# A gated encoder block on one core: z's forms loaded ahead of the last head's y_r, whose share goes out by accumulating stores

## The chip, the cores and the metric

One Trainium2 chip, one of its cores. The metric is the device time of one execution in microseconds: the median of the runs. All times inside an execution are counted from the start of its profiled span. Engines are called by their names or by the profile's short forms: TensorE (PE, with PEld for its weight loads), VectorE (DVE), ScalarE (ACT), GpSimd (POOL), SyncE (SP). Transfers started by POOL go through one queue, emptied in order, that the profile calls software_dynamic; those started by SP go through the one called hardware_dynamic.

## What is computed

One layer of an encoder block on x of 512 tokens by 1024 features, all in float32. Cut to what matters here:

```python
h = rmsnorm(x, g_mix)
xc, gb, gc, q, k, v, g_sw, gate_a, gate_r = split(h @ w_in)
y_a = (gb * dwconv3(gc * xc)) @ w_a_out                     # z = gb * conv
ret = retention(q, k, v)                                    # 4 heads, 512 wide each, both directions
y_r = (groupnorm(ret) * g_ret * silu(g_sw)) @ w_r_out       # 2048 rows: 512 of each head
merged = sigmoid(gate_a) * y_a + sigmoid(gate_r) * y_r
x = x + merged @ w_o
x = x + swiglu(rmsnorm(x))                                  # then a last rmsnorm
```

y_r is a sum over four heads, each of which contributes its own product with 512 rows of `w_r_out`.

## The kernel before

Every float32 operand is split into a high and a low part (`split`: the high part is a rounding copy on ScalarE, L167 or L170; the low part is a subtraction on VectorE, L168 or L171), and every product is three matmuls (high·high, high·low, low·high). The weights pass through the same split on their way: a load on SP into a raw tile (L204, L228), for some a sum of two raw tiles on VectorE (L240), the copy, the subtraction. `take()` hands the next split unit to the product and prefetches the units behind it. The order of all weights is fixed by a list, `PLAN`.

Several products, among them y_a = z · w_a_out, are done by a Strassen-like scheme (`strassen`, L375 to 399): seven products of quarter matrices (24 matmuls of 128x512 each, all at L365), in the order a11, s1, s2, a12, s3, a22, s4. Three pairs of banks are used: `a`, `d` and `b`; a holds a11, then a11 + s2 (s2's product adds to it), and so on. Between them stand copies to SBUF (`snap`, L372, ScalarE): p1 is the copy of a after a11, u2 the one after s2, u3 the one after s3. Each product does its first unit of weights for both tiles of tokens, then its second. The left operands (z's forms: a11, a12, s1 to s4, a22, high and low) were written to DRAM by `z_forms` long before, and are loaded back into tiles of the pool `big` named `zform`.

The heads run in a loop (L802 to 817): the product of scores with v (`do_pv`), a group norm, a transposition on VectorE (`do_t`, L181), and one head late the head's share of y_r, `do_wr(h - 1)`. That is two products (`half` 0 and 1, the left and right 512 columns), each of 48 matmuls (L280 to L282) into four banks. Of heads 0 to 2 each bank is copied to a tile by ScalarE (`snap`) and stored by POOL into `yrd[half]` in DRAM, from head 1 on with `accum_op=ALU.add`, so that the DMA adds to what is there (L788). Ahead of the last head's share the sum so far is loaded (L822), after it z's forms (L827) and the gate of A (`sga`, L832), all by POOL. The gate of R (`sgr`) was loaded by SP (L815). The last head's products are evicted by VectorE (`ev_last`): the bank is added to the sum (L792), which is multiplied by `sgr` (L793). Then comes the y_a product, whose four evictions merge: times `sga` (L840), plus the finished R part (L841). `turn` then transposes a half of the merged rows on TensorE (L851) and splits it, and w_o's product (L280 to L282 again) reads the split.

Three pools matter. `big` has 14 buffers of 1 MB; `tmp` has nine tiles of 128x512, from which every `snap` takes one, and a tile is free again when its last reader is done, for a stored one when the store has landed; PSUM has eight banks. The instructions of an engine run in the order in which a scheduler put them when the kernel was built. A wait at the head of an engine's queue holds all behind it. POOL's transfers use eight counters in turn, and each waits until the transfer that last used its counter has landed.

Of the kernel before, what the change touches and what calls it, by code (L numbers as in the profile page):

```python
# [12 lines left out]
F32 = mybir.dt.float32  # L13
F32R = mybir.dt.float32r
AF = mybir.ActivationFunctionType
ALU = mybir.AluOpType

P = 128
# [4 lines left out]
HEADS = 4  # L23
# [115 lines left out]
def block_kernel(ctx: ExitStack, tc: tile.TileContext, xT, xtok, wpack, wquad, cols, decs, rot, g_ffn, g_final, out):  # L139
    nc = tc.nc  # L140

    const = ctx.enter_context(tc.tile_pool(name="const", bufs=1))
    big = ctx.enter_context(tc.tile_pool(name="big", bufs=14))
# [11 lines left out]
    def bigtile(dt=F32, n=4):  # L155
        return big.tile([P, n, 512], dt, tag="big", name="big", padded_shape=[P, 4, 512])
# [4 lines left out]
    def bank():  # L161
        return psum.tile([P, 512], F32, tag="bank", name="bank")
# [115 lines left out]
    def mm3(ps, left, right, first, last):  # L278
        (lh, ll), (rh, rl) = left, right
        nc.tensor.matmul(ps, lh, rh, start=first, stop=False)  # L280
        nc.tensor.matmul(ps, lh, rl, start=False, stop=False)  # L281
        nc.tensor.matmul(ps, ll, rh, start=False, stop=last)  # L282

    def act_pair(tiles, k, sl=slice(0, S)):
        hi, lo = tiles
        return hi[k // 4][:, k % 4, sl], lo[k // 4][:, k % 4, sl]
# [10 lines left out]
    def token_major(lhs, row0, chunks, evict, before=None):  # L297


        pss = [bank() for _ in range(NB)]  # L300
        n = 4 * chunks
        for kk in range(n):
            if kk % 4 == 0:
                c = Chunk()
            if before:
                before(kk)
            for nb in range(NB):
                mm3(pss[nb], act_pair(lhs, row0 + kk, slice(nb * P, (nb + 1) * P)),
                    c.w(kk % 4, 0, 512), kk == 0, kk == n - 1)
        for nb in range(NB):  # L310
            evict(nb, pss[nb])
# [12 lines left out]
    def fm_quad(forms, ev11, ev21, ev22, ev12):  # L324

        def w():
            return take()[1][0]
        a, d, b = bank(), bank(), bank()
        prod(w(), forms["a11"], a, True)
        p1 = snap(a)  # L330
        prod(w(), forms["s1"], d, True)
        prod(w(), forms["s2"], a, False)
        u2 = snap(a)
        prod(w(), forms["a12"], b, True)
        nc.vector.tensor_tensor(out=p1, in0=b, in1=p1, op=ALU.add)
        ev11(p1)
        prod(w(), forms["s3"], a, False)
        u3 = snap(a)
        nc.vector.tensor_tensor(out=u3, in0=d, in1=u3, op=ALU.subtract)
        ev22(u3)  # L340
        prod(w(), forms["a22"], a, False)
        ev21(a)
        prod(w(), forms["s4"], d, False)
        nc.vector.tensor_tensor(out=u2, in0=d, in1=u2, op=ALU.subtract)
        ev12(u2)
# [55 lines left out]
    def of(pair, o=0):  # L401
        return lambda k, sl: tuple(t[:, k, sl.start + o:sl.stop + o] for t in pair)
# [139 lines left out]
    def kept(name):  # L542
        return dram.tile([P, 4, 512], F32, name=name)
# [5 lines left out]
    gad = [kept(f"ga{j}") for j in range(2)]  # L549
    grd = [kept(f"gr{j}") for j in range(2)]  # L550

    zd = [[dram.tile([P, n, 4, 256], F32, name=f"z{i}{n}{j}") for i in range(2)]
          for j, n in enumerate((2, 2, 2, 1))]
    yrd = [kept(f"yr{j}") for j in range(2)]
# [7 lines left out]
    def store(dst, t):  # L562
        nc.gpsimd.dma_start(dst, t)
# [81 lines left out]
    def conv(m, b, u, c):  # L645

        nc.scalar.activation(c, u[:, 0:512], AF.Copy, scale=wconv[:, 3 * b:3 * b + 1])
        for tap in (1, 2):
            nc.vector.scalar_tensor_tensor(
                out=c, in0=u[:, tap:tap + 512], scalar=wconv[:, 3 * b + tap:3 * b + tap + 1],  # L650
                in1=c, op0=ALU.mult, op1=ALU.add)

    def u_tile():
        u = misctile(2 * 514, "u").rearrange("p (m n) -> p m n", m=2)
        nc.vector.memset(u[:, :, 0:1], 0.0)
        nc.vector.memset(u[:, :, 513:514], 0.0)
        return u

    def z_forms(s, z):

        x1, x2 = z[:, :, 0:256], z[:, :, 256:512]

        def put(j, t):
            n = t.shape[1]
            hl = [t512(F32R)[:, 0:256 * n].rearrange("p (f t) -> p f t", f=n) for _ in range(2)]
            split(t, *hl)
            for d, x in zip(zd[j], hl):
                store(d[:, :, s, :], x.bitcast(F32))
        v, w = (t512().rearrange("p (f t) -> p f t", f=2) for _ in range(2))
        put(0, x1)  # L670
        for o, a, b, op in ((v[:, 0], x2[:, 0], x2[:, 1], ALU.subtract), (v[:, 1], x1[:, 0], x2[:, 0], ALU.subtract),
                            (w[:, 0], v[:, 0], x1[:, 0], ALU.subtract), (w[:, 1], x1[:, 1], w[:, 0], ALU.add)):
            nc.vector.tensor_tensor(out=o, in0=a, in1=b, op=op)
        put(1, v)
        put(2, w)
        put(3, x2[:, 1:2])
# [18 lines left out]
    def halves(t):  # L695
        return t.rearrange("p (m t) -> p m t", m=2)

    def mix_quads():

        c = bigtile().rearrange("p (s m) t -> p s m t", s=2)  # L700
        for s in range(2):
            u, got = u_tile(), {}

            def ev21(ps):
                nc.vector.tensor_tensor(out=u[:, :, 257:513], in0=halves(ps), in1=halves(got["c2"]), op=ALU.mult)

            def ev12(t):
                nc.vector.tensor_tensor(out=u[:, :, 1:257], in0=halves(got["x1"]), in1=halves(t), op=ALU.mult)
            fm_quad(xf, lambda t: got.update(x1=t), ev21, lambda t: got.update(c2=t), ev12)
            for m in range(2):  # L710
                conv(m, 2 * s + m, u[:, m], c[:, s, m])

        def times(s, t):
            def ev(b):
                o = c[:, s, :, t]
                nc.vector.tensor_tensor(out=o, in0=halves(b), in1=o, op=ALU.mult)
            return ev
        fm_quad(xf, times(0, T1), times(0, T2), times(1, T2), times(1, T1))
        for s in range(2):
            z_forms(s, c[:, s])  # L720


    def load(src, dt=F32):
        t = bigtile(dt)
        nc.sync.dma_start(t if dt == F32 else t.bitcast(F32), src)
        return t
# [54 lines left out]
    def do_wr(h, yr):  # L781
        for half in range(2):
            def ev(nb, ps):
                t = snap(ps)
                if h == 0:
                    store(yrd[half][:, nb, :], t)
                else:
                    nc.gpsimd.dma_start(out=yrd[half][:, nb, :], in_=t, accum_op=ALU.add)  # L788

            def ev_last(nb, ps):  # L790
                t = ysum[half][:, nb, :]
                nc.vector.tensor_tensor(out=t, in0=ps, in1=t, op=ALU.add)  # L792
                nc.vector.tensor_tensor(out=t, in0=t, in1=sgr[half][:, nb, :], op=ALU.mult)  # L793
            token_major(yr, 0, 1, ev if h < HEADS - 1 else ev_last)

    mix_quads()
    nxt = load_head(0)
    p = do_scores(nxt[0], nxt[1])
# [2 lines left out]
    yr = None  # L801
    for h in range(HEADS):  # L802
        if h < HEADS - 1:
            nxt = load_head(h + 1)
        do_pv(p, vv, sg)
        t = sg
        if h < HEADS - 1:
            p = do_scores(nxt[0], nxt[1])
            vv, sg = split_v(nxt[2]), nxt[3]
        new = do_t(h, t)  # L810
        if h == 0:
            do_mix(3)
        else:
            if h == HEADS - 1:
                sgr = [load(t) for t in grd]  # L815
            do_wr(h - 1, yr)
        yr = new


    ysum = [bigtile(), bigtile()]  # L820
    for t, d in zip(ysum, yrd):
        nc.gpsimd.dma_start(t, d)  # L822
    zf = {}
    for names, hl in zip((("a11", "a12"), ("s1", "s3"), ("s2", "s4"), ("a22",)), zd):
        t = [big.tile([P, 2, 4, 256], F32R, tag="big", name="zform") for _ in hl]
        for x, d in zip(t, hl):
            nc.gpsimd.dma_start(x[:, 0:len(names)].bitcast(F32), d)  # L827
        for j, n in enumerate(names):
            zf[n] = of([x[:, j] for x in t])
    sga = [bigtile(), bigtile()]  # L830
    for t, d in zip(sga, gad):
        nc.gpsimd.dma_start(t, d)  # L832
    do_wr(HEADS - 1, yr)
    mt = ([], [])


    def merge(half, o):
        def ev(tt, ya):
            t = sga[half][:, o + tt, :]
            nc.vector.tensor_tensor(out=t, in0=ya, in1=t, op=ALU.mult)  # L840
            nc.vector.tensor_tensor(out=t, in0=t, in1=ysum[half][:, o + tt, :], op=ALU.add)  # L841
        return ev

    def turn(half):
# [260 lines left out]
    a, d, b = ([bank(), bank()] for _ in range(3))  # L1105
# [93 lines left out]
```

## Time and profile before

| what | value |
|---|---|
| median of three runs | 1051.09 us (1050.66 to 1052.85) |
| the profiled execution | 1050.25 us |
| its span | 1048.5 us |
| TensorE busy | 1030.8 us (98%) |
| VectorE busy | 877.8 us (84%) |
| ScalarE busy | 520.2 us (50%) |
| POOL's DMA queue | 51.39 MB, 16.4% of 16 engines' span |
| SP's DMA queue | 131.12 MB, 36.9% |

The rows that the prediction shows are of these kinds. A row of a timeline gives start, length, engine, line, operation, tiles, shapes and a count (x4: four in a row, merged), and in brackets the idle time before it and what ended it. A row of the chain gives start, length and what. A row of windows gives the stretch, its length, the busy time and number of instructions of PE, PEld, DVE, ACT and POOL, then the granted clock of TensorE (1.00 is full speed), the busy share of the 16 DMA engines and GB/s. A row of the DMA view gives the queue, its packets, MB and the share of the 16 engines' time that its packets took. Matmuls overlap: one of 128x512 has a length of 0.39 us, but in a dense row they start every 0.227 us.

### The profile page before, as it was taken

The numbers are of one execution on the slowest core, as the hardware profiler recorded it, in microseconds if no ns is written. First come the engines' busy times: TensorE is split into PE (matmuls) and PEld (weight loads), VectorE is DVE, ScalarE is ACT, GpSimd is POOL, SyncE is SP. The second block draws the span as 40 slices with busy tenths as digits, with TensorE's granted clock in tenths as the row PEclk, the third lists the DMA queues.
The fourth block names the chain that finished last, engine by engine and source line by source line (L and its number), as shares of the span: only waits on it lengthen the run. The fifth ranks groups of instructions, "written<-read, shape, count | busy, mean of one in ns | idle before, by whom it ended". The sixth has DMA issues, their size and how long they took to land.

```text
span 1048.5 us, 14888 instructions
## 1 busy us (share of the span) xinstructions
PE 1030.8 (98%) x5664; PEld 897.9 (86%) x5664; DVE 877.8 (84%) x1131; ACT 520.2 (50%) x697; POOL 126.3 (12%) x202
## 2 busy tenths in 40 slices
PE   8999999999999999999999989999999999999996
PEld 7788888888888998888878868889998999899985
DVE  6999786958777888698988987659998999889995
ACT  7546654453656445242532424445555565556553
POOL 0111111111101003202122320000002000110010
PEclk9999999999999999999999999999999999999999
DMA  9636647282645577819647897731319422663322
GB/s 323 233 107 213 218 159 244 91 272 89 217 135 192 183 256 245 315 32 355 239 134 188 198 341 266 241 107 36 91 36 274 124 83 79 187 155 101 121 38 84
DMA packets 52920, 183.46 MB, mean 175 GB/s; under 512 B 6896, under 2 KB 6896, under 8 KB 49264
## 3 DMA queue, kind: packets, MB, share of 16 engines
q1 hardware_dynamic: 36592, 131.12, 36.9%
q0 software_dynamic: 16256, 51.39, 16.4%
q8 instruction: 44, 0.72, 0.3%
q14 instruction: 28, 0.23, 0.1%
HBM read 137.66 MB, written 44.83 MB: 174 GB/s over the span
## 4 chain that ended last, share of the span: by engine, by line
PE 87%; DVE 4%; DMA 3%; issue 2%; ACT 2%; POOL 1%; SPq 0%; POOLq 0%; ACTq 0%; DVEq 0%
PE bank L365 31%; PE bank L321 27%; PE bank L280 10%; PE bank L282 9%; PE bank L281 9%; DMA yr<-t 2%; DMA zform<-z 1%; DMA big<-xT 1%; DVE t L769 1%; DVE wlo L168 1%; DVE bnst L764 0%; ACT whi L167 0%; POOL bnmv L767 0%; DVE big L1099 0%; DVE big L771 0%
## 5 line engine op out<-in xcount | busy, mean ns | idle before, releaser
L167 ACT CAST whi<-raw 128x1024 fp32r<-128x1024 f32 (+1 forms) x281 | 289.0, 1032 | 288.1 <-PE bank L365 74.0
L168 DVE TENSOR_TENSOR wlo<-raw,whi 128x1024 fp32r<-128x1024 f32 (+1 forms) x281 | 335.7, 1202 | 108.5 <-ACT whi L167 107.5
L321 PE MATMUL bank<-xform,whi 128*128 128x256 f32 x1440 | 260.3, 283 | 0.0
L321 PEld LDWEIGHTS bank<-xform,whi 128*128 128x128 f32 x1440 | 224.8, 192 | 0.7 <-ACT t L372 0.6
L321 PE MATMUL bank<-xform,wlo 128*128 128x256 f32 x720 | 203.7, 283 | 0.0
L365 PE MATMUL bank<-whi,big 128*128 128x512 f32 x548 | 172.7, 390 | 0.4 <-DVE big L1117 0.4
L240 DVE TENSOR_TENSOR raw<-raw 128x1024 f32<-128x1024 f32 (+1 forms) x124 | 148.4, 1205 | 1.7 <-DMA raw<-wquad 0.4
L321 PEld LDWEIGHTS bank<-xform,wlo 128*128 128x128 f32 x720 | 138.2, 192 | 0.0
L365 PEld LDWEIGHTS bank<-whi,big 128*128 128x128 f32 x548 | 102.7, 188 | 23.3 <-issue 0.8
L365 PE MATMUL bank<-wlo,big 128*128 128x512 f32 x274 | 106.7, 390 | 0.0
L365 PE MATMUL bank<-whi,xform 128*128 128x512 f32 x320 | 101.0, 389 | 0.0
L280 PE MATMUL bank<-whi,big 128*128 128x512 f32 x240 | 94.6, 396 | 2.6 <-ACT big L170 2.0
L281 PE MATMUL bank<-wlo,big 128*128 128x512 f32 x240 | 94.2, 393 | 0.0
L282 PE MATMUL bank<-whi,big 128*128 128x512 f32 x240 | 93.5, 393 | 0.1
L372 ACT COPY t<-bank 128x512 f32<-128x512 f32 x120 | 68.6, 586 | 37.8 <-PE bank L365 17.2
L280 PE MATMUL bank<-big,whi 128*128 128x512 f32 x224 | 87.1, 389 | 0.0
L281 PE MATMUL bank<-big,whi 128*128 128x512 f32 x224 | 87.1, 389 | 0.0
L282 PE MATMUL bank<-big,wlo 128*128 128x512 f32 x224 | 87.1, 389 | 0.0
L365 PEld LDWEIGHTS bank<-whi,xform 128*128 128x128 f32 x320 | 60.1, 188 | 12.5
L167 ACT CAST big<-t 128x512 fp32r<-128x512 f32 (+1 forms) x60 | 34.7, 580 | 61.8 <-DVE t L743 43.1
L365 PE MATMUL bank<-wlo,xform 128*128 128x512 f32 x160 | 62.2, 389 | 0.0
L365 PEld LDWEIGHTS bank<-wlo,big 128*128 128x128 f32 x274 | 51.4, 188 | 10.4
(175 smaller groups left out, 1416.2 us busy)
## 6 DMA issues: line engine op xcount, KB each, us to landing
raw<-wquad SPq DMA_DIRECT2D x124, 512.0 KB, 4.4
raw<-wpack SPq DMA_DIRECT2D x58, 512.0 KB, 5.2
z<-t POOLq DMA_DIRECT2D x24, 256.0 KB, 5.4
yr<-t POOLq DMA_DIRECT2D x24, 256.0 KB, 7.8
zform<-z POOLq DMA_DIRECT2D x6, 1024.0 KB, 13.0
v<-t POOLq DMA_DIRECT2D x16, 256.0 KB, 4.8
sg<-t POOLq DMA_DIRECT2D x16, 256.0 KB, 3.2
qh<-t POOLq DMA_DIRECT2D x16, 256.0 KB, 2.6
```

The costliest lines, as they stand in the source:

```text
L167: nc.scalar.copy(hi, src)
L168: nc.vector.tensor_tensor(out=lo, in0=src, in1=hi.bitcast(F32), op=ALU.subtract)
L240: nc.vector.tensor_tensor(out=t, in0=t, in1=raws[quad, more, u][:, 0:n], op=ALU.add)
L280: nc.tensor.matmul(ps, lh, rh, start=first, stop=False)
L281: nc.tensor.matmul(ps, lh, rl, start=False, stop=False)
L282: nc.tensor.matmul(ps, ll, rh, start=False, stop=last)
L321: nc.tensor.matmul(o, l[:, c], r[:, k], start=start and s == 0 and k == 0 and i == 0, stop=stop and k == 3 and i == 2, skip_group_check=True)
L365: nc.tensor.matmul(pss[tt], l, r[:, c], start=start and k == 0 and i == 0, stop=stop and k == n - 1 and i == 2, skip_group_check=True)
L372: nc.scalar.copy(t, ps)
L769: nc.vector.tensor_scalar(out=t, in0=ps, scalar1=mv[:, 0:1], scalar2=mv[:, 3:4], op0=ALU.subtract, op1=ALU.mult)
```

## The change

Four things change around the end of the heads' loop.

1. z's forms are loaded by `load_z()`, called in the loop's last pass ahead of `do_wr(2)`, at the place where `sgr` was loaded by SP. The single form a22 now takes one buffer for its high and low part instead of two.
2. The last head's share goes the way of the others: a copy by ScalarE and an accumulating store by POOL. `ev_last` is gone.
3. After the stores of each half, that half of y_r's sum is loaded by POOL (`ysum`). Both gates are loaded by POOL ahead of `do_wr(3)`.
4. The merge has three operations instead of two: the sum times `sgr`, y_a times `sga`, and their sum.

```diff
-            def ev_last(nb, ps):
-                t = ysum[half][:, nb, :]
-                nc.vector.tensor_tensor(out=t, in0=ps, in1=t, op=ALU.add)
-                nc.vector.tensor_tensor(out=t, in0=t, in1=sgr[half][:, nb, :], op=ALU.mult)
-            token_major(yr, 0, 1, ev if h < HEADS - 1 else ev_last)
-
+            token_major(yr, 0, 1, ev)
+            if h == HEADS - 1:
+                ysum.append(bigtile())
+                nc.gpsimd.dma_start(ysum[half], yrd[half])
+
+    def later(src):
+        t = bigtile()
+        nc.gpsimd.dma_start(t, src)
+        return t
+
+    def load_z():
+        out = {}
+        for names, hl in zip((("a11", "a12"), ("s1", "s3"), ("s2", "s4"), ("a22",)), zd):
+            n = len(names)
+            t = [big.tile([P, 2, 4, 256], F32R, tag="big", name="zform") for _ in range(n)]
+            parts = t if n == 2 else [t[0][:, 0:1], t[0][:, 1:2]]
+            for x, d in zip(parts, hl):
+                nc.gpsimd.dma_start(x.bitcast(F32), d)
+            for j, name in enumerate(names):
+                out[name] = of([x[:, j] for x in parts])
+        return out
...
             if h == HEADS - 1:
-                sgr = [load(t) for t in grd]
+                zf = load_z()
             do_wr(h - 1, yr)
...
-    ysum = [bigtile(), bigtile()]
-    for t, d in zip(ysum, yrd):
-        nc.gpsimd.dma_start(t, d)
-    zf = {}
...
-    sga = [bigtile(), bigtile()]
-    for t, d in zip(sga, gad):
-        nc.gpsimd.dma_start(t, d)
+    sga, sgr = [later(t) for t in gad], [later(t) for t in grd]
     do_wr(HEADS - 1, yr)
...
-            t = sga[half][:, o + tt, :]
+            t, r = sga[half][:, o + tt, :], ysum[half][:, o + tt, :]
+            nc.vector.tensor_tensor(out=r, in0=r, in1=sgr[half][:, o + tt, :], op=ALU.mult)
             nc.vector.tensor_tensor(out=t, in0=ya, in1=t, op=ALU.mult)
-            nc.vector.tensor_tensor(out=t, in0=t, in1=ysum[half][:, o + tt, :], op=ALU.add)
+            nc.vector.tensor_tensor(out=t, in0=t, in1=r, op=ALU.add)
```

What the scheduler makes of it is seen in three places. The first is POOL's queue behind head 2's stores of y_r (`yr_257` is the left half, `yr_258` the right; `z_249` to `z_256` are z's forms, `ga` and `gr` the gates). Before:

```order
L788 DMA yr_257<-t_5038 128x512
L822 DMA big<-yr_257 128x2048
L788 DMA yr_258<-t_5107 128x512
L788 DMA yr_258<-t_5110 128x512
L788 DMA yr_258<-t_5113 128x512
L788 DMA yr_258<-t_5116 128x512
L822 DMA big<-yr_258 128x2048
L827 DMA zform<-z_249 128x2048
L827 DMA zform<-z_250 128x2048
```

Now:

```order
L788 DMA yr_257<-t_5049 128x512
L806 DMA zform<-z_249 128x2048
L806 DMA zform<-z_250 128x2048
L806 DMA zform<-z_251 128x2048
L806 DMA zform<-z_252 128x2048
L806 DMA zform<-z_253 128x2048
L806 DMA zform<-z_254 128x2048
L806 DMA zform<-z_255 128x1024
L806 DMA zform<-z_256 128x1024
L788 DMA yr_258<-t_5118 128x512
```

All eight loads of z have moved ahead of the right half's stores, and no load of the sum stands before them. The second place is the end of the same queue. Before:

```order
L827 DMA zform<-z_254 128x2048
L827 DMA zform<-z_255 128x1024
L827 DMA zform<-z_256 128x1024
L832 DMA big<-ga_245 128x2048
L832 DMA big<-ga_246 128x2048
L881 TENSOR_TENSOR ac<-ac,mhalf 128x1 x4
```

Now:

```order
L796 DMA big<-gr_248 128x2048
L788 DMA yr_257<-t_5204 128x512
L788 DMA yr_257<-t_5207 128x512
L788 DMA yr_257<-t_5210 128x512
L788 DMA yr_257<-t_5213 128x512
L788 DMA yr_258<-t_5282 128x512
L788 DMA yr_258<-t_5285 128x512
L788 DMA yr_258<-t_5288 128x512
L792 DMA big<-yr_257 128x2048
L788 DMA yr_258<-t_5291 128x512
L792 DMA big<-yr_258 128x2048
```

Behind the gates' loads stand the last head's eight stores, and the sum's halves are loaded last, the left one behind three stores of the right. The third place is the beginning of the y_a product on ScalarE and VectorE. ScalarE before (`t_5333` and `t_5335` are p1, `t_5403` and `t_5405` u2; the casts are weights):

```order
L372 COPY t_5116<-bank 128x512
L167 CAST whi<-raw 128x1024 x6
L372 COPY t_5333<-bank 128x512
L372 COPY t_5335<-bank 128x512
L167 CAST whi<-raw 128x1024 x4
L372 COPY t_5403<-bank 128x512
```

Now (`t_5282` to `t_5291` are the last head's right half, `t_5340` and `t_5342` p1, `t_5410` u2):

```order
L372 COPY t_5282<-bank 128x512
L372 COPY t_5285<-bank 128x512
L372 COPY t_5288<-bank 128x512
L372 COPY t_5291<-bank 128x512
L167 CAST whi<-raw 128x1024 x2
L372 COPY t_5340<-bank 128x512
L167 CAST whi<-raw 128x1024 x2
L372 COPY t_5342<-bank 128x512
L167 CAST whi<-raw 128x1024 x2
L372 COPY t_5410<-bank 128x512
```

The evictions are now copies of this engine, and p1's second copy has moved behind two casts. VectorE before, from the merge of the first quarter on:

```order
L386 TENSOR_TENSOR t_5335<-bank,t_5335 128x512
L840 TENSOR_TENSOR big<-t_5333,big 128x512
L840 TENSOR_TENSOR big<-t_5335,big 128x512
L841 TENSOR_TENSOR big<-big 128x512 x2
L168 TENSOR_TENSOR wlo<-raw,whi 128x1024 x2
L391 TENSOR_TENSOR t_5481<-bank,t_5481 128x512
L391 TENSOR_TENSOR t_5483<-bank,t_5483 128x512
```

Now (the row with the two `L844` is the right half's first operations on its sum):

```order
L386 TENSOR_TENSOR t_5342<-bank,t_5342 128x512
L845 TENSOR_TENSOR big<-t_5340,big 128x512
L845 TENSOR_TENSOR big<-t_5342,big 128x512
L846 TENSOR_TENSOR big<-big 128x512 x2
L844 TENSOR_TENSOR big<-big 128x512 x2
L168 TENSOR_TENSOR wlo<-raw,whi 128x1024
L391 TENSOR_TENSOR t_5490<-bank,t_5490 128x512
L391 TENSOR_TENSOR t_5492<-bank,t_5492 128x512
```

Where a weight's split followed the merge before, two operations on the sum's right half now stand ahead of it.

More of the change, by code (lines that the diff above doesn't have):

```diff
@@ L788, in ev @@
                     nc.gpsimd.dma_start(out=yrd[half][:, nb, :], in_=t, accum_op=ALU.add)
-            def ev_last(nb, ps):
-                t = ysum[half][:, nb, :]
-                nc.vector.tensor_tensor(out=t, in0=ps, in1=t, op=ALU.add)
-                nc.vector.tensor_tensor(out=t, in0=t, in1=sgr[half][:, nb, :], op=ALU.mult)
-            token_major(yr, 0, 1, ev if h < HEADS - 1 else ev_last)
+            token_major(yr, 0, 1, ev)
[17 more added lines that the diff above has]
+        return out
+    ysum = []
     mix_quads()
@@ L814, in block_kernel @@
             if h == HEADS - 1:
-                sgr = [load(t) for t in grd]
+                zf = load_z()
             do_wr(h - 1, yr)
         yr = new
-    ysum = [bigtile(), bigtile()]
-    for t, d in zip(ysum, yrd):
-        nc.gpsimd.dma_start(t, d)
-    zf = {}
[L824 to L829, printed above, removed]
-    sga = [bigtile(), bigtile()]
-    for t, d in zip(sga, gad):
-        nc.gpsimd.dma_start(t, d)
+    sga, sgr = [later(t) for t in gad], [later(t) for t in grd]
     do_wr(HEADS - 1, yr)
```

## The prediction

> **What bounds the kernel now.** First the page: its head and engine line.
>
> ```profile
> span 1048.5 us, 14888 instructions
> PE 1030.8 (98%) x5664; PEld 897.9 (86%) x5664; DVE 877.8 (84%) x1131; ACT 520.2 (50%) x697; POOL 126.3 (12%) x202
> ```
>
> TensorE is busy 98% of the span, so a change off TensorE can win only its gaps. The profiled execution took 1050.25 us; the median of the runs is 1051.09, 0.84 more, which I add at the end. The second view, the chain of work that ended last, shows where the largest gap lies (start, length, what).
>
> ```profile
> 77.40 38.08 PE bank L365 x168
> ...
> 581.54 8.06 DMA yr<-t
> ...
> 595.99 10.96 DMA yr<-t
> ...
> 607.50 0.56 POOL big L822
> 608.05 0.52 POOL zform L827
> 608.59 9.28 DMA zform<-z
> 617.91 39.52 PE bank L365 x166
> 657.43 1.75 PE bank L851 x16
> ```
>
> Between 581 and 618 the chain leaves TensorE: accumulating stores of y_r, the load of its sum, then z's loads (L827), and only then the y_a product (L365). TensorE's timeline there:
>
> ```profile
> 613.17 0.39 PE L282 MATMUL bank<-whi,big 128*128 128x512 f32 x1
> 615.52 0.47 PE L365 MATMUL bank<-whi,zform 128*128 128x512 f32 x1 [1.97 <-DMA zform<-z]
> ...
> 617.91 1.12 PE L365 MATMUL bank<-whi,zform 128*128 128x512 f32 x2 [1.69 <-DMA zform<-z]
> ```
>
> The last head's product is over at 613.4. The y_a product's 168 matmuls end at 657.43, 44.0 later; 168 such matmuls without a gap take 38.08 (0.227 each). So z's late arrival costs 44.0 − 38.1 = **5.9 us**: two waits of 2.1 and 1.9, and 1.9 in which matmuls ran slowly after them (166 in 39.52 instead of 37.6; the granted clock falls in that stretch, eighth column):
>
> ```profile
> 615.00:622.00 7.00, 4.79 (x13) 3.53 (x14) 4.11 (x6) 0.00 (x0) 1.06 (x2) 0.76 1.00 418
> ```
>
> The last two columns say that the DMA engines are full there, at 418 GB/s. Why z comes late is in POOL's timeline:
>
> ```profile
> 579.50 3.56 POOL L788 DMA_DIRECT2D yr<-t  x4 [2.58 <-ACT t L372]
> 590.46 0.57 POOL L822 DMA_DIRECT2D big<-yr  x1 [7.39 <-PE bank L282]
> 594.36 3.51 POOL L788 DMA_DIRECT2D yr<-t  x4 [3.33 <-ACT t L372]
> 607.50 0.56 POOL L822 DMA_DIRECT2D big<-yr  x1 [9.63 <-DMA yr<-t]
> 608.04 2.23 POOL L827 DMA_DIRECT2D zform<-z  x4
> ```
>
> z's loads stand behind a load that waits for the stores' landing.
>
> **Part one: z's loads go early (gain up to 5.9).** They now follow the four stores of 579.50, at 583.1; the buffers they take were last read by the last head's product with v, over at 569.6:
>
> ```profile
> 569.25 0.39 PE L282 MATMUL bank<-big 128*128 128x512 f32 x1
> ```
>
> What matters now is how long POOL's queue, emptied in order, takes. Three windows of the DMA view give its prices (queue, packets, MB, share of 16 engines), of 580 to 590, of 597 to 607 and of 609 to 627:
>
> ```profile
> q0 software_dynamic: 576, 1.05, 78.6%
> ...
> q0 software_dynamic: 558, 1.01, 56.7%
> ...
> q0 software_dynamic: 1012, 7.30, 97.0%
> ```
>
> A set of four accumulating stores (1.05 MB) costs 7.9 us of all engines when it runs alone and 5.7 beside other traffic; plain loads move 7.30 MB in 17.5 us, 0.417 MB a microsecond. In the changed queue nothing runs alone, so I take 5.7 (1.4 a store) and keep 7.9 for the range. z's forms, 7.34 MB, need 17.6 us from 589.6, where the first set lands: with the weights' part they are in at about 611. The first is needed at 613.4, the others every 5.4 us after, so both waits and the slow stretch go.
>
> **Part two: the last head's stores.** Eight more accumulating stores and the two gates' loads (gr comes from SP's queue) now stand between z and y_r's sum. In order: second set of head 2, ga and gr (4.19 MB), two sets of the last head, the two halves of the sum. Beside them SP loads weights of 0.52 MB:
>
> ```profile
> 591.27 4.16 SPq L228 DMA_DIRECT2D raw<-wquad  x2
> 596.19 32.02 SPq L204 DMA_DIRECT2D raw<-wpack  x2
> ```
>
> That is three before 600 (3.8 us of the engines) and, as the y_a product starts earlier, two more from about 622 (their buffers come free with splits that follow the first product's end at 618.9), of which I count 2.3 us ahead of the point sought. Each of POOL's transfers also waits for the landing of the eighth before it; with up to seven queued that never empties the queue, and POOL has no other work until w_o's end. The first store of the last head then lands at 589.6 + 17.6 (z) + 3.8 + 5.7 (set) + 10.0 (gates) + 2.3 + 1.4 = **630.4**.
>
> Who waits for it? The evictions take tiles from the pool of nine. The pool hands them out in turn. Counted from head 2's first half: four tiles, four, then the last head's four and four, then p1 of the y_a product. p1's second tile is the eighteenth, and its buffer is that of the ninth: the last head's first store. Before, the last head took none. ScalarE's rows of before for p1, and the casts of the new evictions' time:
>
> ```profile
> 602.76 1.05 ACT L167 CAST whi<-raw 128x1024 fp32r<-128x1024 f32 x1 [4.39 <-PE bank L282]
> ...
> 623.46 0.59 ACT L372 COPY t<-bank 128x512 f32<-128x512 f32 x1 [0.28 <-PE bank L365]
> 624.82 0.59 ACT L372 COPY t<-bank 128x512 f32<-128x512 f32 x1 [0.77 <-PE bank L365]
> ```
>
> The eight new copies are hidden: ScalarE idles 4.39 between casts and four take some 2. p1's second copy isn't: it ends at 630.4 + 0.6 = 631.0, and the third product, which adds to the same bank, wants it when its own second tile of tokens begins: 613.4 + two products of 24 matmuls (5.44 each) + six matmuls (1.4) = 625.6. **A new wait of 5.4**, and 1.9 of slow matmuls after it as in before. Queued behind that copy on ScalarE are the casts of the coming weights, which TensorE needs only after it. So the gain of 5.9 is already −1.4.
>
> **Part three: y_r's sum.** After 630.4 the queue still has three stores (4.3), three of the next set (4.3; the first half's load waits for landed stores and so falls behind them), the half's load (1.05 MB, 2.5), the last store (1.4) and three weights (some 2.9): 645.8. Then the second half is issued, which lands 5.2 after its issue in before (all loads of L822):
>
> ```profile
> DMA to landing us min/median/max: 5.2/5.2/5.2
> ```
>
> With 0.5 for POOL: **651.5**. VectorE meets its first operation on that half after the first half's merge: the fourth product ends at 613.4 + 4 × 5.44 + 7.3 = 642.5, six operations of 0.6 follow, so from 646.1 VectorE stands, and behind it in its queue are the splits of the last product's weights. VectorE's rows of before, for the prices:
>
> ```profile
> 640.64 1.28 DVE L386 TENSOR_TENSOR t<-bank,t 128x512 f32<-128x512 f32 x2
> 641.84 1.28 DVE L840 TENSOR_TENSOR big<-t,big 128x512 f32<-128x512 f32 x2
> ...
> 653.83 2.36 DVE L168 TENSOR_TENSOR wlo<-raw,whi 128x1024 fp32r<-128x1024 f32 x2
> 656.10 0.69 DVE L398 TENSOR_TENSOR t<-bank,t 128x512 f32<-128x512 f32 x1
> ...
> 660.25 0.69 DVE L168 TENSOR_TENSOR big<-bank,big 128x512 fp32r<-128x512 f32 x1
> ```
>
> From start to start that is 0.60 for an operation of 512 columns (640.64 to 641.84 is two) and 1.14 for a weight's split (653.83 to 656.10). From 640.64 to the turn's first split at 660.25 VectorE has no gap in before, and that split is what w_o's first matmul with a low part waits for:
>
> ```profile
> 661.08 0.41 PE L282 MATMUL bank<-whi,big 128*128 128x512 f32 x1
> ```
>
> In the change, from the second half's landing up to and with that split stand 22 operations of 512 columns and four splits: 22 × 0.60 + 4 × 1.14 = 17.8. It ends at 651.5 + 17.8 = 669.3 instead of 660.25 + 0.6 = 660.85: **8.4 later**, more than TensorE's own delay. What follows is paced by TensorE, so it stays. The last head's own 16 VectorE operations (602 to 618, 9.6 us) go, worth nothing: nobody waits for them. The third operation of each merge adds eight of 0.60; six lie in the chain above and are counted.
>
> [...]
>
> **Rivals.**
> - *Everything hides* (faster). If a set cost only what its bytes cost as a load, 1.05 / 0.417 = 2.5, the first store would land 3.2 + 0.8 earlier, 626.4: a wait of 1.4, no wait for the sum. VectorE's chain is then 1.3 longer than before (six operations more, two splits moved ahead), so −5.9 + 1.3 + 1.4 = −3.2, and −4.6 where even p1 is in time (before 625.0): 1046.5 to 1047.9. For it: TensorE's waits do go. Against: 56.7% and 78.6%. [...]
> - *Only p1 waits.* If the second half lands by 646.1, the loss is 1.4 + 1.3 = 2.7: 1053.8. It needs the queue 5.4 faster after 630, against the sum of bytes. Chance 0.14.
> - *Sets cost 7.9.* Three sets by 2.2 add 6.6, and a slow stretch of TensorE before w_o another 1.9: up to 1068. For it: a set that starts on an idle queue; against: this queue is never idle. Chance 0.12.
> - That z's loads don't move is excluded by the order.
>
> **How the numbers follow.** Forecast (p1 waits 5.4, the sum's second half decides): 1051.09 + 8.4 = 1059.5, chance 0.64, itself 1056 to 1064: low when the first set is covered by z's packets (2.1 of the 10 us from 580 were free) and a weight less lies in the way, high by half of the 6.6 and the slow stretch. The range 1052 to 1066 takes in the second rival and half of the third, and leaves out the first. Under 0.2% (2.1 us) can't be told from no change here: faster 0.10, the same 0.04, slower 0.86.
>
> **What would show it.** Right: no wait of L365 on z at 613; a copy of L372 to p1 that waits for `yr<-t` until about 631, with the third product behind it; VectorE idle before L844 for a landing at about 651; w_o's first L282 near 669. Wrong: p1's copy at 619, or L844 never idle; then the stores were cheaper than 1.4 each.

## The result and the profile after

The changed kernel takes 1061.75 us (median of 4 runs, 1061.07 to 1063.21), the kernel before 1050.88 (4 runs, 1050.33 to 1052.85): a ratio of 1.0103, 95% interval 1.0091 to 1.0115. The change makes the kernel about 10.9 us slower. The profiled execution took 1061.77, with this head and engine line:

```profile
span 1060.0 us, 14903 instructions
PE 1033.8 (98%) x5664; PEld 899.6 (85%) x5664; DVE 873.2 (82%) x1123; ACT 523.8 (49%) x705; POOL 134.4 (13%) x212
```

TensorE still reads 98%: 11.5 us more span and only 3.0 more busy time. The rest are gaps. These are TensorE's only rows with a gap (in brackets: the gap, and what ended it) from 605 to 690:

```profile
629.23 0.50 PE L365 MATMUL bank<-whi,zform 128*128 128x512 f32 x1 [3.66 <-ACT t L372]
...
655.06 0.80 PE L365 MATMUL bank<-whi,zform 128*128 128x512 f32 x1 [5.12 <-DVE t L391]
...
663.94 0.66 PE L856 MATMUL bank<-ident,big 128*128 128x128 f32 x4 [0.34 <-DVE big L846]
...
665.77 0.47 PE L280 MATMUL bank<-whi,big 128*128 128x512 f32 x1 [0.24 <-DVE t L398]
...
667.57 0.47 PE L280 MATMUL bank<-whi,big 128*128 128x512 f32 x1 [1.10 <-DVE t L398]
...
669.88 0.80 PE L282 MATMUL bank<-whi,big 128*128 128x512 f32 x1 [1.61 <-DVE big L168]
```

No row waits on z: the two waits at 613 to 618 are gone. In their place TensorE stands 3.66 us for ScalarE's copy of p1, and 5.12 ahead of the last product of y_a. The first matmul of w_o with a low part starts at 669.88; before, at 661.08. ScalarE's row shows what the copy waited for (a landing of a store of y_r), and VectorE's rows show where the second gap is from:

```profile
628.59 0.58 ACT L372 COPY t<-bank 128x512 f32<-128x512 f32 x1 [5.97 <-DMA yr<-t]
```

```profile
644.44 1.29 DVE L844 TENSOR_TENSOR big<-big 128x512 f32<-128x512 f32 x2 [7.99 <-DMA big<-yr]
645.65 1.22 DVE L168 TENSOR_TENSOR wlo<-raw,whi 128x1024 fp32r<-128x1024 f32 x1
646.78 1.28 DVE L386 TENSOR_TENSOR t<-bank,t 128x512 f32<-128x512 f32 x2
...
651.98 1.29 DVE L844 TENSOR_TENSOR big<-big 128x512 f32<-128x512 f32 x2 [1.51 <-DMA big<-yr]
653.18 1.22 DVE L168 TENSOR_TENSOR wlo<-raw,whi 128x1024 fp32r<-128x1024 f32 x1
654.32 1.28 DVE L391 TENSOR_TENSOR t<-bank,t 128x512 f32<-128x512 f32 x2
```

L844 multiplies y_r's sum by its gate. VectorE stands 7.99 us for the sum's left half and 1.51 for its right half, and the split of a weight (L168) is queued behind each. L391, which TensorE's last product of y_a waits for, comes behind the second. The chain of work that ended last names the same places (start, length, what):

```profile
613.33 2.73 PE bank L365 x12
616.66 17.70 DMA yr<-t
...
635.54 10.09 DMA yr<-t
...
646.38 5.58 DMA big<-yr
...
669.23 0.61 DVE big L168
669.88 0.80 PE bank L282
...
681.77 1.75 PE bank L856 x16
```

From 616.7 to 652 it runs through the stores of y_r and the load of its sum. The turn of the right half (16 transposes) starts at 681.77; in the chain of before that row is

```profile
670.34 1.75 PE bank L851 x16
```

so the turn is 11.4 later, w_o's first low part 8.8: another 2.6 are lost in between. The windows show how (length, then busy time of PE, PEld, DVE, ACT and POOL; then the granted clock):

```profile
626.00:629.00 3.00, 0.00 (x0) 0.00 (x0) 0.00 (x0) 0.41 (x1) 0.86 (x1) 1.00 1.08 287
629.50:633.00 3.50, 3.50 (x16) 2.84 (x16) 2.23 (x2) 2.26 (x3) 0.00 (x0) 1.00 1.11 268
...
654.65:658.06 3.41, 3.00 (x7) 2.45 (x8) 3.41 (x7) 0.00 (x0) 0.00 (x0) 0.52 0.50 154
664.00:668.00 4.00, 2.66 (x12) 1.60 (x12) 4.00 (x7) 1.36 (x3) 0.00 (x0) 1.00 0.82 248
668.25:675.07 6.82, 5.21 (x13) 4.14 (x13) 6.82 (x10) 0.00 (x0) 0.00 (x0) 0.51 0.93 319
```

After p1's wait the clock stays at 1.00. It is halved for 3.4 us after the 5.12 wait, and for 6.8 us at the start of w_o's product, after a stretch in which TensorE had short gaps and transposes. From 669.88 to 675.07, 5.2 us at half the clock are 2.6 us of work. In the kernel before, w_o's product starts at the full clock:

```profile
660.00:664.00 4.00, 4.00 (x19) 3.13 (x18) 4.00 (x7) 0.46 (x1) 0.00 (x0) 1.00 0.98 374
```

### The profile page after: what moved, and what is told of

Same layout as the page of the kernel before. It is cut to its first block, busy times and chain, and to the rows that moved or that the text cites. A ratio compares the mean times of both kernels' runs of the same rounds, so it can differ in the third digit from the quotient of the medians.

```text
span 1060.0 us, 14903 instructions
## 1 busy us (share of the span) xinstructions
PE 1033.8 (98%) x5664; PEld 899.6 (85%) x5664; DVE 873.2 (82%) x1123; ACT 523.8 (49%) x705; POOL 134.4 (13%) x212
## 4 chain that ended last, share of the span: by engine, by line
PE 85%; DVE 7%; DMA 4%; ACT 2%; issue 1%; POOL 1%; SPq 0%; POOLq 0%; DVEq 0%; ACTq 0%
PE bank L365 27%; PE bank L321 27%; PE bank L282 10%; PE bank L280 10%; PE bank L281 10%; DMA yr<-t 3%; DVE big L181 1%; DVE wlo L168 1%; DVE t L769 1%; ACT whi L167 1%; DMA big<-xT 1%; DMA big<-yr 1%; ACT big L170 1%; DVE bnst L764 0%; DVE big L771 0%
## 5 line engine op out<-in xcount | busy, mean ns | idle before, releaser
L168 DVE TENSOR_TENSOR wlo<-raw,whi 128x1024 fp32r<-128x1024 f32 (+1 forms) x281 | 335.6, 1202 | 113.9 <-ACT whi L167 112.9
L372 ACT COPY t<-bank 128x512 f32<-128x512 f32 x128 | 73.1, 584 | 49.7 <-PE bank L365 16.2
```

The costliest lines, as they stand in the source:

```text
L168: nc.vector.tensor_tensor(out=lo, in0=src, in1=hi.bitcast(F32), op=ALU.subtract)
L372: nc.scalar.copy(t, ps)
```

## The experiments

What is to be told apart: that POOL's queue lands y_r's sum late and VectorE's work behind it sets the end (the prediction's theory); that p1's wait sets it; that the longer merge does; that z's early loads do. The last four runs came out of the first eight. The ratios are to the kernel before.

**The pool of nine made thirteen** (changed kernel; `big` gives up one buffer for it)

```diff
-    big = ctx.enter_context(tc.tile_pool(name="big", bufs=14))
+    big = ctx.enter_context(tc.tile_pool(name="big", bufs=13))
-    tmp = ctx.enter_context(tc.tile_pool(name="tmp", bufs=9))
+    tmp = ctx.enter_context(tc.tile_pool(name="tmp", bufs=13))
```

> The changed kernel with 13 small tiles instead of nine (and 13 big buffers instead of 14), so that p1's second copy takes a tile that has long been free. Theory 1 (the queue: what decides is when POOL's queue has delivered the right half of y_r's sum): the wait of 3.7 us before the third product goes, the sum's right half still lands at about 651 to 652, TensorE waits that much longer ahead of the last product, and the time stays within 1 us of the changed kernel's 1061.7. Theory 2 (the pool of nine is the cost): 3.7 us come back, 1058.

Measured: 1063.72 us, ratio 1.0123 (1.0107 to 1.0139); no gain. p1's second copy is now at 619.83 with no wait for a store, TensorE has no gap before 640, and the time comes back at the sum:

```profile
645.30 1.29 DVE L844 TENSOR_TENSOR big<-big 128x512 f32<-128x512 f32 x2 [11.80 <-DMA big<-yr]
```

VectorE waits 11.80 us there instead of 7.99, to nearly the same point in time (645.30; in the changed kernel 644.44). p1's wait is real and costs the end nothing.

**gr not loaded** (changed kernel)

```diff
-    sga, sgr = [later(t) for t in gad], [later(t) for t in grd]
+    sga = sgr = [later(t) for t in gad]
```

> The changed kernel without the two loads of gate R; the merge multiplies the sum by gate A's tiles instead, so the same number of operations remains and 2.1 MB leave the queue. Theory 1 (the queue): 2.1 MB at 0.417 MB a microsecond are 5.0 us; the sum's right half lands at about 647, p1 does not wait, and the time falls by 5 to 7.5 us (the upper end if the slow matmuls after the last wait go too): 1054 to 1057. Theory 2 (the pool of nine): 3.7, 1058. Theory 3 (the merge's third operation on VectorE is the cost): no change, 1061 to 1062.

Measured: 1058.91 us, 1.0076 (1.0059 to 1.0093): 2.8 won, under what was expected. The queue did what was said: the load of the right half of the sum is issued 7.7 earlier (638.63 against 646.38). But VectorE's instructions come in another order:

```profile
645.74 1.29 DVE L844 TENSOR_TENSOR big<-big 128x512 f32<-128x512 f32 x2 [4.88 <-DMA big<-yr]
646.95 1.22 DVE L168 TENSOR_TENSOR wlo<-raw,whi 128x1024 fp32r<-128x1024 f32 x1
648.09 1.28 DVE L386 TENSOR_TENSOR t<-bank,t 128x512 f32<-128x512 f32 x2
649.29 1.28 DVE L845 TENSOR_TENSOR big<-t,big 128x512 f32<-128x512 f32 x2
```

The multiplication of the right half stands ahead of L386 and the left half's merge; in the changed kernel it stood behind them. So two things change in this run, and its 2.8 is no price of gr. The last run but one keeps that multiplication behind the merge: there VectorE has 16.6 us of work from its first use of the right half to the end of the turn's first split (644.88 to 661.52), here 22.5 (645.74 to 668.26).

**Last head's stores that replace instead of adding** (changed kernel)

```diff
-                if h == 0:
+                if h in (0, HEADS - 1):
                     store(yrd[half][:, nb, :], t)
```

> The changed kernel whose last head stores without accumulating (what is left out: the earlier heads' share of the sum). Theory 1 with the price of the rows (a set of four accumulating stores takes 5.7 us of all engines, by its bytes a plain one 2.5): the sum's right half lands some 6 us earlier and the time falls by 6 to 9, 1053 to 1056. If an accumulating store costs no more than its bytes: no change, 1061 to 1062.

Measured: 1056.77 us, 1.0051 (1.0036 to 1.0066): 5.0 won, somewhat under what was expected. POOL's rows, first of the changed kernel and then of this one (head 2's first set, and the load of the sum's right half):

```profile
579.28 3.55 POOL L788 DMA_DIRECT2D yr<-t  x4 [2.59 <-ACT t L372]
...
646.38 0.56 POOL L792 DMA_DIRECT2D big<-yr  x1 [9.92 <-DMA yr<-t]
```

```profile
580.97 3.56 POOL L788 DMA_DIRECT2D yr<-t  x4 [2.58 <-ACT t L372]
...
643.43 0.54 POOL L792 DMA_DIRECT2D big<-yr  x1 [9.89 <-PE bank L365]
```

Between the two stand 67.1 us with adding stores and 62.5 without: eight stores cost 4.6 more, 0.6 each. Each store moves 256 KB in both, so in this queue adding has a price of its own.

**The merge without the multiplication of the sum** (changed kernel)

```diff
-            nc.vector.tensor_tensor(out=r, in0=r, in1=sgr[half][:, o + tt, :], op=ALU.mult)
```

> The changed kernel without the multiplication of the sum by gate R (left out; the gate is still loaded), so the merge has two operations. Theory 1: the operation that meets the late sum first is then the merge's last one; the split of the last product's first weights and the subtractions no longer stand behind it. After the landing at 652 some 12 operations of 0.6 and three splits of 1.14 are left to w_o's first low matmul instead of 22 and four: 7 us less, 1053 to 1056. Theory 3 (only the operations' own time): six times 0.6, 3.6 less, 1058.

Measured: 1058.82 us, 1.0069 (1.0054 to 1.0084): 2.9 won, less than the prediction's theory gave, and near the 1058 of a rival. VectorE's work behind the sum is shorter, but the sum is later too:

```profile
655.41 1.29 DVE L845 TENSOR_TENSOR big<-big 128x512 f32<-128x512 f32 x2 [4.07 <-DMA big<-yr]
```

That is the first use of the right half (now the addition), at 655.41 instead of 651.98. VectorE stood less earlier on (4.50 us for the left half instead of 7.99), so its splits freed weight buffers sooner, and more loads of weights went beside the queue: from 636 to the landing of the right half SP issues four of them here (at 636.3, 638.5, 647.8 and 649.0), in the changed kernel two (at 636.5 and 646.9). That these loads are what makes the sum later is argued from the rows; no run takes them away.

**z's loads later** (changed kernel: the call moved out of the loop, to stand ahead of the gates)

```diff
-            if h == HEADS - 1:
-                zf = load_z()
             do_wr(h - 1, yr)
...
+    zf = load_z()
     sga, sgr = [later(t) for t in gad], [later(t) for t in grd]
```

> The changed kernel with z's loads written behind head 2's stores again; three of the eight stand ahead of the right half's stores, five behind. Theory 1: the queue carries the same bytes, so the sum's right half lands at 651 to 652 as in the changed kernel; 1060 to 1063. Theory 4 (the early loads of z push the stores back and are the cost): the time falls to 1056 or less.

Measured: 1062.43 us, 1.0113 (1.0100 to 1.0127): as the changed kernel. Five of z's eight loads now follow head 2's right stores; the end does not notice. z's place ahead of those stores is not the cost.

**z's loads alone** (kernel before; its merge, its stores and gr as they were; `load_z(lo, hi)` loads the groups lo to hi of z's four groups of forms, a22 in one buffer as in the change)

```diff
                 sgr = [load(t) for t in grd]
+                load_z(0, 4)
             do_wr(h - 1, yr)
...
+    for d in yrd:
+        ysum.append(bigtile())
+        nc.gpsimd.dma_start(ysum[-1], d)
```

> The kernel before with all of z's loads moved ahead of head 2's right stores and nothing else (gate R by SP, the last head added by VectorE to the loaded sum). Theory 1: the sum's left half now falls behind 7.3 MB of z and a set of stores and lands at about 619 instead of 596; VectorE, which needs it at 602, stands until then, and with it the split of the y_a product's weights: TensorE waits some 10 us from 613, less the 5.9 that z no longer costs: 1055 to 1060. Theory 5 (only the last head's stores are the cost, z's early loads are a gain by themselves): 1045 to 1046.

Measured: 1053.29 us (10 runs), 1.0023 (1.0013 to 1.0034): slower, but by less than expected. The wait for z is gone and another has its place, since in this method VectorE adds the sum to the last head's banks before TensorE may use them again:

```profile
619.96 0.77 PE L365 MATMUL bank<-whi,zform 128*128 128x512 f32 x1 [5.46 <-issue]
```

```profile
619.16 1.29 DVE L792 TENSOR_TENSOR big<-bank,big 128x512 f32<-128x512 f32 x2 [1.02 <-DMA big<-yr]
```

TensorE's matmul starts 0.8 after VectorE's first addition, which waited for y_r's sum. That this addition is what ended the wait is read from the times: the profile names nothing ("issue"). One wait of 5.46 stands for two of some 2: here too what is last in POOL's queue is waited for.

**The old method, with the queue in another order** (kernel before: of z, the two loads of a11 and a12 go early, right behind head 2's left stores; then come the left half of the sum, the right stores, the right half of the sum and the rest of z; in the second version s1 and s3 go early too)

```diff
                 sgr = [load(t) for t in grd]
+                load_z(0, 1)
...
             token_major(yr, 0, 1, ev if h < HEADS - 1 else ev_last)
+            if h == HEADS - 2:
+                ysum.append(bigtile())
+                nc.gpsimd.dma_start(ysum[half], yrd[half])
...
-    ysum = [bigtile(), bigtile()]
-    for t, d in zip(ysum, yrd):
-        nc.gpsimd.dma_start(t, d)
...
+    load_z(1, 4)
```

> The kernel before with the queue in the order of need: the left stores, the two loads of a11, the sum's left half, the right stores, the sum's right half, then the other forms of z; the last head is added by VectorE as before. Theory 1: left half lands at about 598 (needed at 602), right half at about 612 (613), a11 at 595 (613), s1 at 617 (619), s2 at 622 (624): all in time, the 5.9 us of before go and nothing takes their place: 1045 to 1046. If the queue is slower than that by 2 us, s1 and the right half are late by as much: 1047.

> As the kernel with a11 early, but s1 and s3 stand ahead of the sum's left half too. Theory 1: 4.2 MB ahead of the left half instead of 2.1, so it lands at about 604 and the right half at about 616, 3 us after VectorE needs it; the split of s1's weights stands behind: some 3 of the 5.9 us are given back, 1048. If the order inside the queue does not matter, the same as the other: 1045.

Measured: 1045.80 us, 0.9957 (0.9944 to 0.9969), and 1045.69 us, 0.9951 (0.9939 to 0.9964), beside 1050.55 for the kernel before on the same chip. Both beat both kernels, and the second isn't worse than the first, as had been expected. In the first, TensorE has one gap left between 605 and 700, and in the second none:

```profile
619.91 0.73 PE L365 MATMUL bank<-whi,zform 128*128 128x512 f32 x2 [0.84 <-DMA zform<-z]
```

So z's waits, predicted at 5.9, were worth having: 4.8 and 4.9 come from the order of the queue alone. Of the versions that leave nothing out, these two are the only ones here that are faster than the kernel before.

**Two costs, then three, taken out together** (changed kernel: replacing stores and no multiplication; then gr not loaded besides). The diffs are those above.

> The changed kernel with two of its costs taken out together: the last head's eight stores replace instead of adding (what the earlier heads had summed is overwritten), and the merge has no multiplication of y_r's sum. Alone they gave 5.0 and 2.9 us. Theory A (queue and VectorE act in series: what the queue lands earlier and what VectorE then has to do add up): 1061.5 - 5.0 - 2.9 = 1053 to 1054. Theory B (the shorter merge only moves VectorE's wait, so that with earlier landings it is worth more than alone): 1050 to 1052. Theory C (one of them hides the other): 1056 to 1057.

> As the run before, and the gates of the right branch are not loaded either (those of the left are used in both places). With this the queue carries neither the price of adding nor a load more than before. Theory A (series): 1053.5 - 2.8 = 1050 to 1051. Theory B (queue and merge are the whole loss, and once no wait is left the gain of z's early loads shows): 1045 to 1048, with no wait of VectorE for y_r's sum. Theory C: 1054 or more, so that a further cost is in the change.

Measured: 1051.24 us (10 runs), 1.0000 (0.9983 to 1.0016), and 1044.63 us, 0.9940 (0.9924 to 0.9957). The two together give 10.5, where 5.0 and 2.9 make 7.9. That surplus is not clear of the noise (0.17% by the four ratios, about 0.3% either way). The rows point the same way: VectorE waits 2.86 us for the sum's right half here and not at all for its left, where with the shorter merge alone it waited 4.07 and 4.50. With all three out, TensorE has no gap from 600 to 690, and the kernel is 0.6% faster than before. Within what these runs can tell, the loss is made of these three, and the gain is of the size of z's waits; what each of them costs by itself does not follow, since alone they gave 5.0, 2.9 and 2.8, and together 17.1.

**gr in SP's queue again** (changed kernel; nothing left out)

```diff
             if h == HEADS - 1:
+                sgr = [load(t) for t in grd]
                 zf = load_z()
...
-    sga, sgr = [later(t) for t in gad], [later(t) for t in grd]
+    sga = [later(t) for t in gad]
```

> The changed kernel, with gr loaded by SP's queue ahead of the last head, as in the kernel before, and all else as changed: the same bytes, in another queue. Theory 1 (the landing of y_r's sum behind POOL's queue sets the end; gr's 2.1 MB cost that queue 5.0 us, of which leaving them out altogether gave 2.8): 1058 to 1060. Theory 2 (what counts is the bytes in flight at once, not the queue): 1061 to 1062.

Measured: 1052.69 us (10 runs), 1.0014 (1.0004 to 1.0025): 9.1 won where 2 to 4 were expected. The direction was right; the size had been taken from the run with gr left out, whose order of VectorE had spoilt it. The windows from 564 to 580, of before, of the changed kernel and of this one (the last two columns: share of the DMA engines, and GB/s), say what gr costs where:

```profile
564.00:580.00 16.00, 16.00 (x72) 13.24 (x71) 12.45 (x24) 2.43 (x5) 4.29 (x7) 1.00 0.99 293
```

```profile
564.00:580.00 16.00, 16.00 (x72) 13.24 (x72) 12.61 (x24) 2.53 (x4) 4.28 (x8) 1.00 0.66 161
```

```profile
564.00:580.00 16.00, 16.00 (x73) 13.24 (x71) 12.58 (x24) 2.44 (x5) 4.30 (x7) 1.00 0.97 292
```

SP moves gr while the DMA engines would be idle a third of the time, at no cost to TensorE, which is busy for all 16 us in each row; POOL moves it some 44 us later through the queue that the sum waits in. The edit changes queue and time together, and no run tells the two apart. In this run the rows of that queue, of VectorE and of TensorE read:

```profile
639.30 0.56 POOL L792 DMA_DIRECT2D big<-yr  x1 [11.21 <-PE bank L365]
```

```profile
636.59 2.50 DVE L845 TENSOR_TENSOR big<-big 128x512 f32<-128x512 f32 x4 [7.18 <-DMA big<-yr]
...
644.88 1.29 DVE L845 TENSOR_TENSOR big<-big 128x512 f32<-128x512 f32 x2
```

```profile
647.96 0.50 PE L365 MATMUL bank<-whi,zform 128*128 128x512 f32 x1 [1.86 <-DVE t L391]
...
661.58 0.80 PE L282 MATMUL bank<-whi,big 128*128 128x512 f32 x1 [1.61 <-DVE big L168]
```

The right half's load is issued 7.1 earlier and VectorE doesn't wait for it at all (644.88, no bracket); p1's wait is gone from TensorE's rows. What is left is VectorE without a gap from 636.6 to past w_o's first matmul with a low part, at 661.58: 8.3 earlier than in the changed kernel, and still not ahead of before. Of the 8.3, 7.1 are the earlier use of the right half. The other 1.2 are two multiplications of the left half that the scheduler has put ahead of it (x4 at 636.59, where the changed kernel has x2), so this run too has another order on VectorE, if a lesser change. And w_o's product again begins at half the clock:

```profile
660.00:667.00 7.00, 5.42 (x13) 4.26 (x14) 7.00 (x10) 0.00 (x0) 0.00 (x0) 0.55 0.93 324
```

**The same, with the merge's multiplication left out**

> The run before (gr by SP's queue) with the merge's multiplication of y_r's sum left out besides. In the run before VectorE has no gap from its first multiplication of the sum at 636.6 us to past the turn's first split at 660.8, so it is VectorE that sets the turn there. Theory V (the third operation of the merge is what is left of the loss): eight operations of 0.60 us lie in that chain, and the slow matmuls ahead of w_o's product go with TensorE's last waits: 1052.7 - 4.8 - 2 = 1045 to 1048, what the two versions by the old method with z's first forms early gave. Theory Q (the queue still sets the end): 1051 or more.

Measured: 1051.44 us (10 runs), 1.0007 (0.9993 to 1.0021). The theory that the third operation was all that was left falls: 1.3 less, which is within the spread of these runs, instead of some 6. As in the other run without it, the sum came later:

```profile
632.38 7.96 DMA raw<-wquad
640.33 0.23 issue
640.57 7.10 DMA big<-yr
...
659.00 0.61 DVE big L168
659.66 0.80 PE bank L282
```

In this chain the load of the right half is issued 1.3 later than in the run before and takes 7.10 us to land, behind a load of weights; VectorE waits for it until 647.8. Queue and VectorE lie some 4 us apart here (a wait of 4.28), so taking from one brings out the other. The slow stretch at w_o's start, which this theory took to be gone, is still there: the clock is 0.74, 0.50 and 0.91 in the windows 656 to 660, 660 to 664 and 664 to 668, which puts it at about 657.9 to 664.7.

## Why the prediction was right, and where its sizes were off

The forecast of 1059.5 us in the range 1052 to 1066 met 1061.75, by the mechanism it named. Its steps:

- *z's gain of 5.9.* Right, or a little high. No wait on z is left. The order of the queue alone gave 4.8 and 4.9, and without its three costs the changed kernel is 0.60% faster than before (0.43 to 0.76%, or 4.5 to 8.0 us).
- *5.7 for a set of adding stores.* Somewhat high: eight stores cost 4.6 more than plain ones, where the sum had 2 × (5.7 − 2.5) = 6.4.
- *Each of POOL's transfers waits for the eighth before it, in a queue emptied in order.* As said. In the changed kernel the first two stores of the right half start at 619.23 and 622.17, after 1.71 and 2.08 us of waiting for ga's two loads, which stand eight places ahead; the left half's first store, which was issued behind the gates' loads, landed after them, at about 628.5.
- *p1's wait of 5.4, and 1.9 of slow matmuls.* The wait came by that path, the pool's ninth buffer, but is 3.66, since the first store landed at about 628.5 and not 630.4. The clock didn't fall behind it (1.00 from 629.5 to 633.0). The step that follows ("so the gain of 5.9 is already −1.4") was of no weight for the end; with thirteen buffers the time is no better.
- *The right half lands at 651.5.* Right: VectorE starts on it at 651.98. That it came so close is luck, since errors cancelled in the queue: the first store landed 1.9 early, and from there to the issue of the right half's load it took 17.9 (628.5 to 646.4) instead of 15.4.
- *17.8 us of VectorE from there to the turn's first split, 669.3.* Right: 651.98 to 669.84.
- *"What follows is paced by TensorE, so it stays."* This is the term that was mis-sized: 0 for the likeliest case, 2.6 measured. After waits and transposes TensorE began w_o's product at half its clock (0.51) for 6.8 us. The prediction had such a stretch, at 1.9, only in the third rival and in the upper end of its range. 1059.5 and these 2.6 make 1062.1.
- *The gates' loads.* 10.0 us for both was one term of the queue among others. gr's half of it turned out to be nearly the whole loss: 9.1 by the medians and 8.1 between the two profiled spans, which the queue's 7.1 and VectorE's 1.2 above account for. The 3.4 us slow stretch goes with it; the one of 6.8 at w_o's start stays, and p1's wait, which goes too, was of no weight. The text didn't say that one of the two had been free before, in SP's queue at a time when the DMA engines were idle.

Of the rivals, the one in which everything hides is out by the 7.99 and the 1.51, "only p1 waits" by the run with thirteen buffers, and sets at 7.9 by the run with replacing stores: two of them would cost 2 × (7.9 − 2.5) = 10.8 more than plain ones, where 4.6 were measured. Open stays why the queue was quicker than predicted up to the first store and slower behind it: no run separates the packets of loads and stores within it.

## What to carry to other kernels

On a queue whose transfers land in the order of their issue, as ga's two loads and the store behind them did here, what is put ahead of the one transfer that is waited for can cost its full time and more (gr's 2.1 MB: 5.0 us by its bytes at 0.417 MB a microsecond, 7.1 in the queue, 9.1 in the kernel); move a load into it only after a look at whether its old place was free. Price a step by an experiment that leaves the order of every engine's instructions alone, or compare that order first: a removed load that lets a waiting instruction slip forward in VectorE's queue hid 6 of 9 us here. Where two limits lie close together, don't add up what each change gave alone: 5.0, 2.9 and 2.8 were 17.1 together.

## What the runs showed of the hardware

The length of TensorE's gap didn't decide whether its clock fell. A gap of 3.66 us left it at 1.00 in the changed kernel (the windows above), and after one of 2.46 in the run with replacing stores it was halved:

```profile
646.00:649.00 3.00, 3.00 (x15) 2.47 (x14) 1.56 (x4) 1.05 (x1) 0.00 (x0) 1.00 0.97 404
649.58:652.05 2.47, 0.01 (x2) 0.00 (x1) 2.47 (x5) 1.04 (x1) 0.00 (x0) 1.00 0.00 0
652.60:656.00 3.40, 3.40 (x10) 2.65 (x9) 3.40 (x5) 0.00 (x0) 0.00 (x0) 0.54 0.42 147
```

The slow stretches were 3.4 or 6.8 us long, and 13.7 in the run with the shorter merge (worked out from its windows of 4 us: 0.80, 0.50, 0.50, 0.50 and 0.99 from 656 to 676): one, two or four of the same length. In the changed kernel the clock falls at 654.8 and 668.45 (in the windows 654.5 to 655.0 and 668.0 to 668.5 it is 0.80 and 0.95), 13.65 us or four such lengths apart. Nor did TensorE's busy time in a stretch of that length: by the lengths of its rows it is busy for 0.00 of the 3.45 us from 625.65 to 629.10, within the gap of 3.66, and the clock stayed at 1.00; of the 3.45 us from 665.0 to 668.45 it is busy for 1.93, and then the clock fell:

```profile
625.65:629.10 3.45, 0.00 (x0) 0.00 (x0) 0.00 (x0) 0.51 (x2) 0.86 (x1) 1.00 1.08 280
665.00:668.45 3.45, 1.93 (x7) 0.69 (x5) 3.45 (x7) 0.36 (x1) 0.00 (x0) 1.00 0.87 258
```

No run moved a gap on purpose, so what decides whether the clock falls was not shown.
